# Two routed expert layers: smaller blocks of rows for the least used experts, experts sorted by count in both layers, and weight units of two neighbouring rows per partition

## The chip, the cores and the metric

One core of one Trainium2 chip runs the whole program as one launch. The metric is the device time of one execution in microseconds (us), the median of the runs. Three runs of the kernel before gave 2294.69 us (2292.59 to 2294.75).

## The reference

A diffusion backbone of two layers on 512 latent tokens and 256 context tokens of 1024 features. Layer 0 has a mixer of gated linear recurrence and differential attention, layer 1 one of windowed attention; each is followed by a mixture of 16 experts, of which every token takes two. Layer 0's experts see all 768 tokens, layer 1's the 512 latent ones. The change is in the experts:

```python
def routed_moe(h2d, router_w, router_b, w_gate, w_up, w_down):
    ...
    wts = wts / jnp.sum(wts, axis=-1, keepdims=True)
    ...
    def expert_block(args):
        xblk, e = args
        hid = jax.nn.silu(xblk @ w_gate[e]) * (xblk @ w_up[e])
        return hid @ w_down[e]

    yb = lax.map(expert_block, (xb, block_e)).reshape(n_rows, d_)
    out = jnp.zeros((n_tok + 1, d_), F32).at[row_tok].add(yb * row_w[:, None])
    return out[:n_tok]
```

All numbers are float32. Each of an expert's three weights is 1024 x 1024, 4 MB, so a layer's experts have 201 MB of weights. How many tokens an expert gets depends on the data and is known on the chip only after the router. The result is `x + g2 * f`, and after layer 1 a norm over the features.

## The kernel before, in words

**Precision.** The experts' float32 products are made of three products of parts: `split` (L170 to L197) takes a raw weight from DRAM apart into a high part of 12 bits (ScalarE, L190) and the rest (VectorE, L192), `parts` (L1179) does the same with tokens (`xh`, `xl`) and hidden values (`hh`, `hl`), and `mm3` (L204) issues the products high x high, high x low and low x high, one matmul each (L205 to L207).

**Slots and blocks.** The experts of a layer stand in 16 slots. A slot has room for one block of 128 rows (tokens), or for two. `slot_plan` (L38) gives layer 0 two slots of two blocks, 5 and 11, so 18 blocks; expert 0 always has slot 0, and the others are ranked by their counts on the chip, the two largest in the slots of two blocks. In layer 1 slot s is expert s, with one block each. What doesn't fit in a slot's rows goes to overflow blocks, run by a loop on the device (`For_i`, L1691) whose count comes from the data. A block always takes all of its 128 rows through the matmuls, however many are tokens.

**Steps.** A slot has twelve steps, one for each unit of weights of 1 MB (`load`, L1224). Steps 0 to 3 are gate, gate, up, up for the left 512 columns of the hidden features, 4 to 7 the same for the right 512; such a unit has four groups of 128 rows and 512 columns, a row of 2 KB for each. Steps 8 to 11 are the down weights, two groups of 128 rows and 1024 columns. Each step has twelve matmuls of 512 columns for each block, four for each of the three products, 144 in a slot of one block. The loop over the steps is written so that a unit is split while the one before is multiplied. What follows a product is put off to later steps by a table `late`: `at(step, False, fn)` for the vector engines, `at(step, True, fn)` for TensorE. So the silu product of a half (`hidden`, L1242) is computed in the step after, its four transposes come behind that step's matmuls, and its parts one step later. A block's tokens are fetched from DRAM by an indirect DMA in GpSimd's queue (`fetch`, L1158, `gather`, L1197), transposed by TensorE (`transpose4`, L1173, matmul on L1176) and split. A block's result is weighted and stored to the table YD in DRAM by GpSimd's queue (`result`, L1313, store on L1324), one row of 1024 for each place of a block.

**Loads.** Raw units lie in rings of buffers of 1 MB (strings FIRST and ROUND name the pool that each unit takes). In layer 0, 11 buffers go round, in layer 1, 15. SyncE issues the loads in order (L161), each as soon as its buffer is free. AHEAD lists the units that are loaded before the first tokens are known: twelve of slot 0, and in layer 1 three of slot 1, on GpSimd's queue.

**Ends.** The results of all slots but the last are picked up for each token by indirect gathers from YD (`fetch_y`, L1110), in layer 0 two gathers for each of two early tiles of 128 tokens into `ye` (multiplied by the gate on L1683, added to the stream on L1687), in layer 1 two for each of four tiles that add straight into the stream `xs`. The last slot's block (`direct`, L1284) goes to its tokens without YD: a matmul with a matrix of ones at the tokens' places (`pick`, P on L1280), L1305, is added to the stream on L1306. In layer 1 each tile is then normed and written out (`finale`, L1264). Rows of YD that no slot writes, the overflow's, are set to zero during layer 0's mixer by 14 stores of 512 KB from a small tile `z` (L770).

## Time and profile before

| | |
|---|---|
| runs before | 2294.69 us, the median of 3 (2292.59 to 2294.75) |
| the profiled execution's span, first to last instruction | 2290.2 us |
| TensorE (PE) busy | 2132.9 us, 93% of the span, 11809 matmuls |
| VectorE (DVE) busy | 1702.7 us, 74% |
| ScalarE (ACT) busy | 1381.4 us, 60% |
| GpSimd (POOL) busy | 202.4 us, 9% |
| moved by DMA | 571.26 MB, mean 249 GB/s |
| mean granted TensorE clock | 0.970 |
| splits of weights on DVE (L192) | 822 of 1217 ns, 977.0 us |

The profile is one execution. Times of stages are from the span's start; the runs' median is 4.5 us above this span. Averages over the span hide that the two expert parts have limits of their own, so the stages are read apart. "Busy" of PE counts matmuls, PEld loads of the matmul's stationary operand, which run beside them. A clock of 1.00 is TensorE's upper level of 2.4 GHz, 0.50 its lower level of 1.2 GHz.

### The profile page before, as it was taken

The page shows a single profiled execution, that of the slowest core. Times are in us where ns is not written, and L with a number is a line of the kernel's source. Part 1 is how long each engine was busy: PE and PEld are TensorE (multiplying, and loading weights), DVE is VectorE, ACT ScalarE, POOL GpSimd, SP SyncE. Part 2 cuts the span into 40 slices and gives each one's busy share as a digit, 9 for nine tenths or more (in the row PEclk, how much of TensorE's full clock was granted, in tenths as well). Part 3 has the DMA queues.
Part 4 walks back from the last instruction along what each step waited for, and adds up shares of the span by engine and source line. Part 5 has one row for each costly group of instructions (what it writes and reads, how often), then busy time and mean ns, then how long its engine had stood idle before and what let it go on. Part 6 is the DMA issues. An engine that isn't in the chain of part 4 may idle for free.

```text
span 2290.2 us, 32247 instructions
## 1 busy us (share of the span) xinstructions
PE 2132.9 (93%) x11809; PEld 1717.3 (75%) x11809; DVE 1702.7 (74%) x2506; ACT 1381.4 (60%) x2069; POOL 202.4 (9%) x248
## 2 busy tenths in 40 slices
PE   4899999998969999999999789999979999999997
PEld 2777899996748878888888567566758877777775
DVE  3566646657789975999579865565589988888896
ACT  5344574443348764888478652565368777777774
POOL 2011020000100000000000320000110000000003
PEclk8899999999979999999999899999989999999998
DMA  8556332213689995999699552330489999999985
GB/s 312 199 183 219 87 96 80 75 39 99 227 305 361 375 370 196 380 390 387 225 332 381 185 153 111 148 130 1 167 340 392 388 373 371 372 370 367 375 298 119
DMA packets 244029, 571.26 MB, mean 249 GB/s; under 512 B 12438, under 2 KB 48160, under 8 KB 237720
## 3 DMA queue, kind: packets, MB, share of 16 engines
q1 hardware_dynamic: 215024, 480.24, 57.6%
q0 software_dynamic: 21728, 73.78, 9.8%
q10 hardware_dynamic: 7112, 15.10, 2.0%
q8 instruction: 96, 1.57, 0.3%
q14 instruction: 69, 0.57, 0.1%
HBM read 532.26 MB, written 36.81 MB: 248 GB/s over the span
## 4 chain that ended last, share of the span: by engine, by line
PE 78%; issue 8%; DVE 6%; ACT 4%; DMA 3%; POOL 1%; ACTq 0%; DVEq 0%; SPq 0%; POOLq 0%
PE acc L207 20%; PE acc L205 20%; PE acc L206 20%; PE tp L1176 3%; PE po L1087 2%; PE acc L245 2%; PE big L1021 2%; DVE wl L192 2%; PE acc L1073 1%; PE pair L662 1%; ACT wh L190 1%; PE acc L697 1%; PE acc L647 1%; POOL rr L150 1%; PE big L552 1%
## 5 line engine op out<-in xcount | busy, mean ns | idle before, releaser
L192 DVE TENSOR_TENSOR wl<-raw,wh 128x1024 fp32r<-128x1024 f32 (+1 forms) x822 | 977.0, 1217 | 166.3 <-ACT wh L190 150.6
L190 ACT ACTIVATE wh<-raw 128x1024 fp32r<-128x1024 f32 (+1 forms) x822 | 848.2, 1054 | 276.8 <-PE acc L207 239.2
L205 PE MATMUL acc<-wh,xh 128*128 128x512 f32 x1088 | 437.5, 403 | 0.0
L206 PE MATMUL acc<-wl,xh 128*128 128x512 f32 x1088 | 436.1, 401 | 0.9 <-DVE wl L192 0.8
L207 PE MATMUL acc<-wh,xl 128*128 128x512 f32 x1088 | 432.1, 397 | 0.0
L207 PE MATMUL acc<-wh,hl 128*128 128x512 f32 (+2 forms) x888 | 331.7, 376 | 12.9 <-DVE hl L1181 11.0
L205 PE MATMUL acc<-wh,hh 128*128 128x512 f32 (+2 forms) x888 | 328.0, 381 | 3.9 <-ACT hh L464 3.9
L206 PE MATMUL acc<-wl,hh 128*128 128x512 f32 (+2 forms) x888 | 331.0, 375 | 0.0
L206 PEld LDWEIGHTS acc<-wl,xh 128*128 128x128 f32 x1088 | 206.1, 189 | 52.8 <-DVE wl L192 7.4
L207 PEld LDWEIGHTS acc<-wh,xl 128*128 128x128 f32 x1088 | 205.9, 189 | 48.1 <-DVE xl L1181 0.5
L205 PEld LDWEIGHTS acc<-wh,xh 128*128 128x128 f32 x1088 | 205.8, 189 | 47.0 <-ACT xh L1180 0.5
L207 PEld LDWEIGHTS acc<-wh,hl 128*128 128x128 f32 x888 | 167.8, 190 | 45.3 <-DVE hl L1181 15.8
L205 PEld LDWEIGHTS acc<-wh,hh 128*128 128x128 f32 x888 | 169.2, 191 | 29.0 <-ACT hh L464 4.3
L206 PEld LDWEIGHTS acc<-wl,hh 128*128 128x128 f32 x888 | 168.4, 191 | 28.3 <-DVE wl L192 3.6
L1160 POOL DMA_INDIRECT xg<-H,rowi x32 | 43.9, 1370 | 615.5 <-PE tp L1176 552.9
L150 POOL TENSOR_TENSOR rr<-rv,mhalf 128x1 f32<-128x1 f32 (+1 forms) x54 | 39.1, 724 | 487.9 <-DVE rv L148 470.2
L1026 DVE TENSOR_REDUCE mx<-big 128x1 f32<-128x512 f32 (+1 forms) x64 | 48.1, 756 | 37.1 <-PE big L1024 36.4
L1180 ACT ACTIVATE xh<-tp 128x512 fp32r<-128x512 f32 x68 | 38.9, 588 | 50.2 <-PE tp L1176 30.1
L1028 ACT ACTIVATE ex<-big,mx 128x512 f32<-128x512 f32 (+1 forms) x64 | 47.2, 738 | 33.2 <-DVE mx L1027 32.9
L205 PE MATMUL acc<-hh,wh 128*128 128x384 f32 x192 | 66.5, 346 | 0.8 <-DVE ya L705 0.8
L1180 ACT ACTIVATE hh<-tp 128x512 fp32r<-128x512 f32 x68 | 39.6, 588 | 43.3 <-PE tp L1176 43.3
L206 PE MATMUL acc<-hl,wh 128*128 128x384 f32 x192 | 65.5, 341 | 0.0
(397 smaller groups left out, 3097.5 us busy)
## 6 DMA issues: line engine op xcount, KB each, us to landing
raw<-in_moe_w_up_dram SPq DMA_DIRECT2D x127, 1024.0 KB, 7.7
raw<-in_moe_w_down_dram SPq DMA_DIRECT2D x127, 1024.0 KB, 7.0
raw<-in_moe_w_gate_dram SPq DMA_DIRECT2D x126, 1024.0 KB, 7.9
raw<-in_ada_w_dram SPq DMA_DIRECT2D x48, 1024.0 KB, 6.5
YD<-y POOLq DMA_DIRECT2D x33, 512.0 KB, 6.8
raw<-in_even_w_in_dram SPq DMA_DIRECT2D x40, 256.0 KB, 4.7
YD<-z POOLq DMA_DIRECT2D x14, 512.0 KB, 12.5
raw<-in_even_w_in_dram SPq DMA_DIRECT2D x12, 512.0 KB, 4.2
```

The costliest lines, as they stand in the source:

```text
L150: G.tensor_tensor(r, v, mhalf[:, :n], OP.pow)
L190: S.activation(v[0], src, AF.Copy)
L192: newest[0] = V.tensor_sub(v[1], src, v[0].bitcast(FT))
L205: T.matmul(o, xh, wh, start=start, stop=False)
L206: T.matmul(o, xh, wl, start=False, stop=False)
L207: T.matmul(o, xl, wh, start=False, stop=stop)
L245: T.matmul(ps[32 * i:32 * i + 32], cT[:, k], raw[:, 0, 512 * i:512 * i + 512], start=k % burst == 0, stop=k != kb and k % burst == burst - ...
L1021: T.matmul(ps[:, o0:o1], qT, kT[:, x, k0:k0 + o1 - o0], start=x == 0, stop=x == 1 and not ms, skip_group_check=True)
L1026: V.tensor_reduce(mx[:, i:i + 1], ps[:, :n], AX.X, OP.max, negate=True)
L1028: S.activation(e[:, :n], ps[:, :n], AF.Exp, scale=0.125, bias=mx[:, i:i + 1], accum_out=sm[:, i:i + 1])
L1176: T.transpose(pt[:, i], src[:, 128 * i:128 * i + 128], ident)
L1180: S.activation(oh, pt, AF.Copy)
```

## The change

**Sizes.** A class Plan takes for each slot the number of rows of its blocks. Layer 0: fourteen slots have a block of 128, of which slots 5 and 11 have a further one of 32 rows instead of 128; slots 8 and 15 have 64 rows alone. Layer 1: slots 0, 1, 2, 4, 6, 8, 10, 12, 14 have 128 rows, slots 3, 5, 7, 9, 11, 13 and 15 have 64. In both layers the experts but 0 are ranked by their counts.

**Thin blocks.** A block of 64 or 32 rows isn't split. Its tokens and the raw weights are multiplied in float32, one matmul instead of three, and two (or four) matmuls for different columns of the weights stand side by side in TensorE's array (`thin`, `tile_position`). A slot that is thin alone has twelve steps of one unit each, gate 0 to 3, up 4 to 7, down 8 to 11, and no split; its hidden values (`hidden_thin`) are computed at the end of step 7 at once and not put off. Its result is stored in two or four pieces (`store_rows`). A table of the row's tokens and weights that is repeated for the pieces (`again`) comes from one matmul per size.

**Units.** A unit is now 256 rows by 1024 columns of a weight, with two neighbouring rows on one partition, 8 KB in one run. A whole slot's gate and up steps take halves of the columns of two units each, so all eight units are used in steps 0 to 3 and again in steps 4 to 7. To match, the transposes take every second column (`turned` in place of `transpose4`).

**Order.** Layer 1 loads ahead only slot 0's twelve units; each further slot's expert is read by SyncE from the sorted list. The zeroing of YD covers the thin blocks' rows too, as one store and 21 copies from the rows that it cleared. In layer 0 the blocks' tokens have two buffers instead of three.

```diff
-SLOTS = [slot_plan(2), (None, [1] * 16)]
-AHEAD = [(range(11), range(11, 12)), (range(12), range(12, 15))]
+AHEAD = [(range(11), range(11, 12)), (range(12), range(0))]
...
+PLANS = [
+    Plan([(128,)] * 5 + [(128, 32)] + [(128,)] * 2 + [(64,)] + [(128,)] * 2 + [(128, 32)] + [(128,)] * 3 + [(64,)]),
+    Plan([(128,)] * 3 + [(64,), (128,)] * 6 + [(64,)]),
+]
...
-                    for i in range(min(nbs), max(nbs) + OVMAX):
-                        G.dma_start(YD[128 * i:128 * i + 128, :].rearrange("p (a b) -> p a b", a=4), z[:, None, :].to_broadcast([128, 4, 256]))
+                    clear = sorted(thin | set(range(min(nbs), max(nbs) + OVMAX)))
+                    G.dma_start(YD[128 * clear[0]:128 * clear[0] + 128, :].rearrange("p (a b) -> p a b", a=4), z[:, None, :].to_broadcast([128, 4, 256]))
+                    def clear_next(n):
+                        for b in clear[1 + 2 * n:3 + 2 * n]:
+                            G.dma_start(YD[128 * b:128 * b + 128, :], YD[128 * clear[0]:128 * clear[0] + 128, :])
...
+                def turned(src):
+                    m, k = src.shape[0], src.shape[1] // 128
+                    pt = tp([128, k, m])
+                    v = src.rearrange("p (u x j) -> p u j x", x=128, j=2)
+                    for i in range(k):
+                        T.transpose(pt[:, i], v[:, i // 2, i % 2], ident[:m, :m])
...
+                def thin(ps, x, w, start, stop):
+                    m = x.shape[1]
+                    n = 8 * m
+                    for r in range(128 // m):
+                        T.matmul(ps[m * r:m * r + m, :n], x, w[:, n * r:n * r + n], start=start, stop=stop, tile_position=(0, m * r))
...
-                        w = (wg, wu, wd)[q // 2 % 2 if q < 8 else 2]
-                        w = w[ds(e, 1)].rearrange("o (k p) n -> p (o k) n", p=128)
-                        if q < 8:
-                            return unit(w[:, 4 * (q % 2):4 * (q % 2) + 4, 512 * (q // 4):512 * (q // 4) + 512], i, eng, order)
-                        return unit(w[:, 2 * (q - 8):2 * (q - 8) + 2, :], i, eng, order)
+                        w = (wg, wu, wd)[q // 4][ds(expert(s), 1)].rearrange("o (u p j) n -> p (o u) (j n)", p=128, j=2)
...
+                        rs = [unit(12 * s + 4 * m + 2 * kh + x) for x in range(2)]
+                        return [w for r in rs for w in split(r[:, :, 512 * c:512 * c + 512])], rs
...
+                    def hidden_thin(p, step):
+                        pg, pu = p["ps"]
...
+                        if step is None:
+                            vec()
+                            turn()
+                            store()
...
+                                elif p["m"] < 128 and q == (3 if whole else 7):
+                                    if whole:
+                                        hidden_thin(p, i + 1)
                                     else:
+                                        at(i, True, lambda p=p: hidden_thin(p, None))
...
-                    if one:
-                        base, top = C("base1"), C("top1")
+                    es_ = tt(inner(rank), outer(C(f"order{li}")), OP.is_equal, q3)
+                    V.tensor_copy(esi, red(tt(es_, inner(e16), OP.mult, q3), OP.add, q2))
...
-                        slots.append((e, [r // 128 for r in rows], [slice(r, r + 128) for r in rows]))
-                    gen = run(slots)
+                    gen = run([(lambda s=s: nc.sync.value_load(esi[0:1, s:s + 1], min_val=0, max_val=15)) if s else 0 for s in range(16)],
+                              plan.blocks, plan.sizes)
```

**The order of the instructions, at three places.** On SyncE, which issues the loads, where layer 1's experts begin (`raw` is a buffer of a unit; the names behind the arrow are the weights in DRAM). Before:

```order
L161 DMA raw<-in_moe_w_gate_dram 128x4x512 x2
L161 DMA raw<-in_moe_w_up_dram 128x4x512 x2
L161 DMA raw<-in_moe_w_gate_dram 128x4x512 x2
L161 DMA raw<-in_moe_w_up_dram 128x4x512 x2
L161 DMA raw<-in_moe_w_down_dram 128x2x1024 x4
```

And now:

```order
L158 DMA raw<-in_moe_w_gate_dram 128x2048 x4
L158 DMA raw<-in_moe_w_up_dram 128x2048 x4
L158 DMA raw<-in_moe_w_down_dram 128x2048 x4
L1726 TENSOR_LOAD esi
L1726 ISA x2
```

The four gate units come ahead of the four up units, each with one run per partition, and slot 1's expert number is read from the sorted list (`esi`) before its first load.

On TensorE in layer 1, where before one slot's work runs on (`xh`, `xl`: a block's tokens in parts; `sg`: the silu product; `tp`: a transpose's target). Before:

```order
L205 MATMUL acc<-wh,xh 128x512
L206 MATMUL acc<-wl,xh 128x512
L207 MATMUL acc<-wh,xl 128x512
L1176 MATMUL tp<-ct,sg 128x128 x4
L205 MATMUL acc<-wh,xh 128x512
```

And now, over a thin slot between two whole ones (`xn`, `hn`: its tokens and hidden values, `xg` with a number: the next block's tokens):

```order
L204 MATMUL acc<-wh,hl 128x512
L1203 MATMUL acc<-raw,xn 64x512 x32
L1185 MATMUL tp<-ct,xg_16381 128x128 x4
L1185 MATMUL tp<-ct,sg 128x128 x4
L1203 MATMUL acc<-raw,hn 64x512 x4
L1185 MATMUL tp<-ct,xg_16381 128x128 x4
L1203 MATMUL acc<-raw,hn 64x512 x12
L202 MATMUL acc<-wh,xh 128x512
```

A thin slot is 48 matmuls from raw weights in place of 144 from split ones; the transposes of `sg` stand right ahead of the matmuls that need them, with none of its own slot's between.

On VectorE at the end of layer 0's experts (`ye`: results gathered for an early tile; `y`: the last slot's rows; names with a number are the stream's tiles and gates). Before:

```order
L1254 TENSOR_TENSOR sg<-sg,acc 128x512
L192 TENSOR_TENSOR wl<-raw,wh 128x1024 x3
L1181 TENSOR_TENSOR hl<-tp,hh 128x512
L192 TENSOR_TENSOR wl<-raw,wh 128x1024 x2
L1683 TENSOR_TENSOR ye<-ye,g_12052 128x1024 x2
L1293 SCALAR_TENSOR_TENSOR y<-acc,roww,g_12052 128x512 x2
```

And now:

```order
L189 TENSOR_TENSOR wl<-raw,wh 128x1024 x2
L1371 TENSOR_SCALAR P<-ct,again_5964 128x128 x2
L1795 TENSOR_TENSOR ye<-ye,g_11691 128x1024 x2
L1334 TENSOR_TENSOR sg<-sg,acc 128x512
L1195 COPY hn<-tp 128x2x2x64
L1388 SCALAR_TENSOR_TENSOR y<-acc,again_5964,g_11691 64x512 x2
```

Before, the products of `ye` stand behind the last slot's splits; now, with no split in that slot, they stand ahead of its silu product.

## Rows read from the trace of the kernel before

**Rows 1.** Windows: stretch, length, busy us by engine, clock, DMA share, GB/s.
```profile
core 0: us, PE busy (x) PEld busy (x) DVE busy (x) ACT busy (x) POOL busy (x), PEclk, DMA share, GB/s
...
650.00:1300.00 650.00, 642.86 (x2896) 519.97 (x2897) 540.89 (x539) 470.18 (x525) 37.43 (x42) 0.99 0.90 330
1682.00:2222.00 540.00, 529.98 (x2395) 424.22 (x2395) 487.92 (x482) 405.55 (x447) 31.88 (x29) 1.00 1.01 376
1700.00:1800.00 100.00, 100.00 (x463) 81.77 (x462) 93.65 (x92) 79.79 (x87) 7.52 (x7) 1.00 1.03 392
```

**Rows 2.** Instructions by line and shape: count, busy us, mean ns, idle before.
```profile
L205 PE MATMUL acc<-wh,xh 128*128 128x512 f32 x1088 | 437.5, 403 | 0.0
...
L1176 PEld LDWEIGHTS tp<-ct,xg 128*128 128x128 f32 x272 | 35.1, 145 | 21.1 <-issue 12.3
```

**Rows 3.** SyncE's timeline in layer 0: start, duration, loads of down weights.
```profile
832.77 10.35 SPq L161 DMA_DIRECT2D raw<-in_moe_w_down_dram  x4
...
937.81 8.73 SPq L161 DMA_DIRECT2D raw<-in_moe_w_down_dram  x4
...
973.02 8.71 SPq L161 DMA_DIRECT2D raw<-in_moe_w_down_dram  x4
```

**Rows 4.** The same in layer 1, with the last loads.
```profile
1877.28 9.29 SPq L161 DMA_DIRECT2D raw<-in_moe_w_down_dram  x4
...
1914.07 9.29 SPq L161 DMA_DIRECT2D raw<-in_moe_w_down_dram  x4
...
2215.08 2.64 SPq L161 DMA_DIRECT2D raw<-in_moe_w_down_dram  x2
```

**Rows 5.** TensorE's timeline: float32 matmuls of other parts; L1305 is of full width.
```profile
1417.29 3.64 PE L245 MATMUL acc<-raw,cT 128*32 128x512 f32 x32 [0.51 <-DVE rp L334]
...
1473.37 1.51 PE L1087 MATMUL po<-at,vt 128*64 128x256 f32 x10
...
2267.22 7.13 PE L1305 MATMUL acc<-y,P 128*128 128x512 f32 x16 [0.39 <-DVE y L1293]
```

**Rows 6.** Timeline of layer 1's experts, start and end, four engines.
```profile
1675.74 0.42 DVE L1493 TENSOR_TENSOR q<-r,ct 128x256 f32<-128x256 f32 x1
...
1681.58 0.79 PE L205 MATMUL acc<-wh,xh 128*128 128x512 f32 x1
...
2231.68 0.53 POOL L1324 DMA_DIRECT2D YD<-y  x1 [36.23 <-DVE y L1321]
...
2235.79 1.65 POOL L1110 DMA_INDIRECT xs<-YD,dse  x1 [3.04 <-DMA YD<-zero]
...
2252.12 1.77 POOL L1110 DMA_INDIRECT xs<-YD,dse  x1 [0.30 <-issue]
...
2275.63 0.68 DVE L1306 TENSOR_TENSOR xs<-xs,acc 128x512 f32<-128x512 f32 x1
```

**Rows 7.** Timeline of GpSimd and VectorE at the end of layer 0's experts.
```profile
1265.89 0.53 POOL L1324 DMA_DIRECT2D YD<-y  x1 [34.66 <-ACT y L1323]
...
1279.96 1.68 POOL L1110 DMA_INDIRECT ye<-YD,dse  x1 [1.24 <-DMA ye<-YD,dse]
...
1294.93 2.35 DVE L1683 TENSOR_TENSOR ye<-ye,g 128x1024 f32<-128x1024 f32 x2
```

**Rows 8.** DMA issues: count, KB each, median us from issue to landing.
```profile
YD<-z POOLq DMA_DIRECT2D x14, 512.0 KB, 12.5
...
ye<-YD,dse POOLq DMA_INDIRECT x4, 6.7
...
xs<-YD,dse POOLq DMA_INDIRECT x8, 7.8
```

**Rows 9.** Windows: the start, while modulation weights of 8 KB per partition are loaded.
```profile
14.00:22.00 8.00, 5.99 (x38) 5.75 (x39) 2.92 (x5) 8.00 (x12) 1.65 (x3) 1.00 1.01 427
```

**Rows 10.** DMA queues, 1700 to 2200 us: packets, MB, share of 16 engines.
```profile
q0 software_dynamic: 3989, 14.52, 7.8%
```

**Rows 11.** Windows: 10 us after TensorE had stood idle.
```profile
100.00:105.00 5.00, 2.84 (x10) 2.24 (x11) 1.41 (x3) 2.34 (x5) 0.00 (x0) 0.50 0.02 3
105.00:110.00 5.00, 5.00 (x37) 2.34 (x37) 2.96 (x4) 1.45 (x4) 0.35 (x1) 0.88 0.30 74
```

More of the change, by code (lines that the diff above doesn't have):

```diff
@@ L1222, in gather @@
                         at(first, False, get)
-                        for q in range(2):
+                        for q in range(2 if m == 128 else 1):
                             at(step + q, True, lambda q=q: turn(q))
                             at(step + 1 + q, False, lambda q=q: store(q))
-                    jobs = [(e, [dict(row=r, x=x) for x, r in enumerate(rows)], bs) for e, bs, rows in slots]
-                    ahead = {}
-                    def weights(i):
-                        return split(ahead.pop(i) if i in ahead else load(i))
@@ L1234, in load @@
-                    def load(i, eng=nc.sync, order=False):
-                        s, q = divmod(i, 12)
-                        e = jobs[s][0]
+                    slots, n = [], 0
+                    for s in range(len(experts)):
+                        slots.append([])
+                        for b, m in zip(blocks[s], sizes[s]):
+                            r0 = (b + NB) * 128 if in_loop else b * 128
+                            row = (lambda i, k, r0=r0: ds(r0, 128)) if in_loop else (lambda i, k, r0=r0: slice(r0 + i, r0 + i + k))
+                            slots[-1].append(dict(b=b, m=m, n=n, row=row))
+                            n += 1
@@ new lines, in part, with unit @@
+                    def part(m, kh, c):
+                        w = (wg, wu)[m][ds(expert(0), 1)].rearrange("o (u p j) n -> p (o u) j n", p=128, j=2)
+                        raw = room[1 + one].tile([128, 2048], FT, name="raw", tag="raw").rearrange("p (k n) -> p k n", k=4)
+                        for x in range(2):
+                            nc.sync.dma_start(raw[:, 2 * x:2 * x + 2], w[:, 2 * kh + x, :, 512 * c:512 * c + 512])
+                        return raw
+                    def unit(u):
+                        if u not in raws:
+                            raws[u] = ahead.pop(u) if u in ahead else load(u)
+                        return raws[u]
@@ L1249, in vec, with hidden @@
+                    def hidden(p, c, step):
+                        pg, pu = p["ps"]
                         def vec():
                             if c == 0:
-                                blk["h"] = [(wk2 if blk["x"] else wk).tile([128, 8, 128], FR, name=x, bufs=1) for x in ("hh", "hl")]
+                                p["h"] = [wk.tile([128, 8, 128], FR, name=x, bufs=1) for x in ("hh", "hl")]
                             sg = wk.tile([128, 512], FT, name="sg", bufs=1 if one else 2)
@@ L1296, in vec, with store_rows, direct @@
+                    def store_rows(p, y):
+                        if p["m"] == 128:
+                            G.dma_start(YD[p["row"](0, 128), :], y)
+                        else:
+                            for _, rows, at_, cs in pieces(p):
+                                G.dma_start(YD[p["row"](0, p["m"]), cs], y[rows, at_])
+                    def direct(p, step):
+                        def vec():
+                            p["y"] = gated(p)
                             if not one:
-                                G.dma_start(YD[blk["row"], :], y2)
@@ L1371, in run @@
-                            for blk in blocks:
-                                if q in (3, 7):
-                                    hidden(blk, c, i + 1)
+                            last = s == len(slots) - 1
+                            split_, as_is = ws
+                            for p in ps_:
+                                if q in (0, 4, 8) and p["m"] == 128 or q == 0:
+                                    p["ps"] = [acc(), acc()]
+                                elif q == 8:
+                                    p["ps"] = [acc()]
@@ L1376, in run @@
                                 elif q == 11:
-                                    (direct if last else result)(blk, i + 1)
+                                    (direct if last else result)(p, i + 1)
                             ws = nws
@@ L1485, in tl @@
                         if n == 256:
-                            return rp.tile(shape, dt, name="q3", bufs=1 if one else 3)
+                            return rp.tile(shape, dt, name="q3", bufs=3)
                         if n in (16 * nt, 96) and not hold:
@@ L1652, in ffn @@
                     next(gen)
+                for m in sizes:
+                    rep = wk.tile([128, 512], FT, name="rep", tag="sg", bufs=1 if one else 2)[:, :128]
+                    V.tensor_copy(rep.rearrange("p (r m) -> p r m", m=m), ident[:, None, :m].to_broadcast([128, 128 // m, m]))
+                    pd = tp([128, 2, NB])
+                    T.matmul(pd, rep, tab, start=True, stop=True)
+                    V.tensor_copy(again[m], pd)
                 if BRIEF[li]:
```

327 lines of the change are left out of this document (180 added, 147 removed).

## The prediction

> **What bounds the kernel now.** I read the busy time by stage first, then the counts, then SyncE's timeline, whose loads mark the pace of the expert slots. The two expert stages are more than half of the span: layer 0's from 655 to about 1300 us, layer 1's from 1682 us to the end. In both TensorE is busy nearly throughout at a clock of 1.00, and in layer 1 the DMA engines are too, at 376 GB/s [rows 1]. The 1088 matmuls of one kind on gathered tokens are 34 blocks of 32: 18 blocks of 128 rows in layer 0 and 16 in layer 1, and no overflow block [rows 2]. A slot of one block takes 35.2 us in layer 0 (973.02 less 937.81) and up to 36.8 us in layer 1 (1914.07 less 1877.28); the stretch from 832.77 to 937.81 holds a two-block slot and a single one, so two blocks take 105.0 - 35.2 = 69.8 us [rows 3, 4]. TensorE sets these times. The DMA engines are close behind it: a slot moves 12.6 MB of weights and 1.05 MB of tokens and results, 36.3 us at 376 GB/s. So a cheaper slot helps only down to the time of its loads, and what the change does to the loads counts as much as what it does to the matmuls.
>
> **No overflow after the change.** From the reference's inputs I worked out the tokens of each expert. Layer 0: expert 0 has 110, the others in order 145, 129, 113, 112, 110, 105, 98, 95, 88, 87, 83, 80, 76, 55, 50. The new slots hold 128 for expert 0, then 160, 160, eleven times 128, and 64, 64. Layer 1: 21, then 122, 106, 98, 94, 82, 71, 69, 69, 53, 50, 46, 45, 35, 34, 29, for nine slots of 128 (expert 0's among them) and seven of 64. All fit.
>
> **A thin slot's matmuls.** A unit of 256 rows by 1024 columns takes 12 matmuls now. For 64 rows it takes four in float32, two side by side; for 32 rows eight of half the width, four side by side. Two rows show the price of such work. 32 float32 matmuls of 512 columns, four side by side, took 3.64 us, and ten of 256 columns, two side by side, 1.51 us; a full-width float32 one took 7.13/16 = 0.45 us [rows 5]. So 512 columns cost 3.64/8 = 0.45 us by the first, 2 x 1.51/5 = 0.60 by the second, and the same 0.45 where nothing stands beside them. A 64-row unit is two such pairs, 0.9 to 1.2 us; I take 0.95, nearer to the row with as many columns, so 11.4 us for a slot of 12 (upper end 14.4). To this come an estimated 3.4 us in which TensorE waits for silu, product and transposes between steps 7 and 8, which here are not put off (the like of it takes 0.4 to 0.8 us each in the rows: 0.68 for a vector instruction of 512 columns [rows 6], 0.59 for four transposes at 145 ns [rows 2]). Together 14.8 us against 35.2. A 32-row block costs about half, 5.2 us, plus an estimated 0.8 for its transposes.
>
> **Layer 0.** The two slots of two blocks become 35.2 + 6 = 41.2 us: 2 x (69.8 - 41.2) = **57 us** less. Slot 8 falls to 14.8 us, but the next whole slot needs eight units in its first four steps, and at some 2.6 us each (below) these come 26 us after slot 8 starts; of the 20 us I keep **10** (ends 4 and 15). Slot 15 gains little. VectorE's order there puts the products of the early tiles (ye) ahead of this slot's own silu product, since no split follows that would hold them back. The ye gathers were queued behind slot 14's store at 1265.89, the fourth was issued at 1279.96 and landed some 7 us later, and the products ran at 1294.93 [rows 7, 8]. Now VectorE stands until about 23 us after slot 14's end, and the slot takes 23 + 2.4 + 3 + 3.6 = 32 us: **2 us** less (up to 14 if the gathers land sooner). The 14 whole slots have as many matmuls as before. Together **69 us**.
>
> **The loads.** Now a partition reads 2 KB runs (gate, up) or 4 KB (down); then every unit is one run of 8 KB per partition. The trace of before has that shape: the modulation weights. While they alone were loaded, the engines moved 427 GB/s at a share of 1.01, against 376 at the same share in layer 1 [rows 1, 9]. I take 427 for weights: 29.5 us per slot. Of the other traffic, 7.8% of 500 us went to 14 slots' gathers and results, 2.8 us each [rows 10]; seven of 16 slots now move half, so 2.2 us. Sum 31.7 us, **2.64 us per unit**. Lower end: no gain from longer runs, 392 GB/s for everything, the rate where the queue was fullest [rows 1]: 13.4 MB per slot, 2.85 us per unit. A page of the Trainium skill, DMA: Bandwidth & Descriptors (section Where 436 GB/s comes from), says that for loads from HBM the HBM side binds at about 358 GB/s. By it a slot takes 37.4 us, estimated from that figure, layer 1 would gain only some 15 us, and the time would be about 2213 us. The trace disagrees: it shows 376, 392 and 427.
>
> **Buffers.** A whole slot now reads its eight gate and up units twice, in steps 0 to 3 and 4 to 7, and frees them only from step 3 on. In layer 0 the ring has 11 buffers: the next slot's eight units can be asked for 12 to 24 us after this slot's start and take 21 us, so the last is there by some 36 us; it is needed 41 us after. In layer 1 there are 15. So I cost holding at nothing; the cover is those 5 us.
>
> **Layer 1.** Experts are sorted there now, so slot 1's units wait for the sorted list instead of being loaded ahead by GpSimd, and about ten vector instructions like the one at 1675.74 stand before expert 0's tokens are split: 0 to 6 us, I take 2; the first matmul moves from 1681.6 to 1683.6 [rows 6]. Slots 0 to 2 are whole, 35.2 to 36.8 us each: until 1791.6. The ring then allows units up to 50; 141 are left. Thirteen slots, seven thin: matmuls need 6 x 36 + 7 x 14.8 = 320 us, loads 141 x 2.64 = 372. So the loads bind and end at 2164, against 2222 [rows 1, 4]. Slot 14's eighth unit is the 16th from the end, 2122; a split and nine steps later the slot ends, about 2151. The tail is next late: slot 14's store was issued at 2231.68, eight adding gathers went out from 2235.79 to 2252.12 and landed some 8 us later [rows 8], about 28 us after the store, hidden under the last slot's 35 us [rows 6]. Now that slot is short and the gathers are not covered: its store goes out at 2153, and 28 us later is 2181; I add 9 us, two thirds of the 13 us of loads that are still under way then, since the gathers share the DMA engines with them: 2190. From the last tile's sum to the end it is 2290.2 - 2275.6 = 14.6 us. The end comes at 2205: **85 us** less.
>
> **Small terms.** Transposes now load every second column: 0 if the weight load still hides (145 ns each [rows 2]), 38 us if it doubles and all shows (17 matmul-bound slots, 16 each, 0.14 us). I take 0, as in the rows that load runs beside the matmul before it. The zeroing of the result table was 14 stores of 12.5 us [rows 8]; now one store and 21 copies in GpSimd's queue during the mixer, where the DMA engines have room (the share was 0.30 at 105 us [rows 11]): 0. At worst one step waits for one landing of that size, 12.5 us; at best one that waited for a store before no longer does, 12.5 us the other way.
>
> **Sum.** 69 + 85 = 154; 2290.2 - 154 = 2136 us of span. The median of the runs, 2294.69, lies 4.5 us over that span: **2140 us**.
>
> **Rivals.**
> *Loads get no faster* (2.85 us per unit): loads end 30 us later, slot 9 loses 3: 2173. For: the longer run is shown in 8 us of the trace only, with little else going on. Against: rate per share is plain there.
> *The clock drops.* Thin slots leave TensorE idle in pieces; after such a stretch it was granted 0.50, its lower level of 1.2 GHz, from 100 to 105 us and 0.88 over the next 5 us of full work [rows 11]. If each whole slot behind a thin one (seven) does its first four steps at that level and one more: at most 4 us each beyond the pace of the loads, 28 in all, 2168. The Trainium skill, TensorE: Matmul & The Clock Gate (section HAM oscillation — how this bites in real kernels), describes the same: a matmul loop that waits for DMA in every round starts every round at the lower clock. No stretch of this trace has such a loop at full length.
> *Pieces do not run side by side*: a 64-row slot costs 21 us, still under its loads, but layer 0 loses 2 x 16 + 10: 2182. Rows 5 speak against it.
> *Everything a little better*: loads at the highest share, gathers unhindered: 2115.
> *Held buffers starve the loads* (slower): if the next slot's eight units come late, each of the 23 whole slots waits. From 6.7 us per slot (154/23) the change loses; at 10 us it gives 2370. That needs 4 us or more per unit where rows 1 show 2.8.
> *The change doesn't do what it says*: an expert over its slot costs a further block, some 45 us: 2185. The counts speak against it.
>
> **Chances.** Forecast 0.52 (its own range 2115 to 2170), slower loads 0.20, clock 0.12, better 0.05, not side by side 0.03, overflow 0.03, starved loads 0.05. The range 2105 to 2215 takes in all but the starved loads, some of the best case, and the transposes' upper end on top of a rival. Below 0.2% (4.6 us) a measurement can't tell a difference; faster 0.94, same 0.01, slower 0.05.
>
> **What would show it.** Right: slots 5 and 11 of layer 0 at 41 us; thin slots of layer 1 with TensorE waiting for loads, a pair of whole and thin at 63 us; 420 GB/s or more there; ye's products ahead of slot 15's silu product in layer 0, and some 20 us at the end in which the gathers are awaited. Wrong: whole slots over 37 us in layer 0 (held buffers, transposes), a rate at 390, a clock of 0.5 through whole slots, or an overflow block.

## The result, and the profile after

| | before | after |
|---|---|---|
| median of the runs, same chip (4 each) | 2293.64 us | 2198.69 us (2195.63 to 2201.97) |
| ratio | | 0.9589, 95% interval 0.9574 to 0.9604 |
| span of the profiled execution | 2290.2 us | 2197.3 us |
| first product of layer 0's experts | 655.60 | 653.13 |
| last slot's product with P, layer 0 | 1298.30 | 1257.22 |
| first product of layer 1's experts | 1681.58 [rows 6] | 1642.06 |

The marks that no row ahead shows, on TensorE's timeline, of the kernel before:

```profile
655.60 0.79 PE L205 MATMUL acc<-wh,xh 128*128 128x512 f32 x1
...
1298.30 3.70 PE L1305 MATMUL acc<-y,P 128*128 128x512 f32 x8 [0.16 <-DVE y L1293]
```

And of the changed kernel:

```profile
653.13 0.79 PE L202 MATMUL acc<-wh,xh 128*128 128x512 f32 x1
...
1257.22 2.77 PE L1418 MATMUL acc<-y,P 64*128 64x512 f32 x8 [0.85 <-DVE y L1388]
...
1642.06 0.79 PE L202 MATMUL acc<-wh,xh 128*128 128x512 f32 x1
```

The change gains 95 us where 154 were forecast: faster, inside the range, with a time 59 us above the forecast. By the marks of the table, layer 0's experts went from 642.7 to 604.1 us, **38.6 us** less (forecast 69); layer 1's, up to the end of the span, from 608.6 to 555.2 us, **53.4 us** less (forecast 85). What lies ahead of the experts and between the layers moved by 2.5 us less and 1.6 more.

The costliest groups of the page after, part 5 (busy us, mean ns of one), answer to [rows 2]:

```profile
L202 PE MATMUL acc<-wh,xh 128*128 128x512 f32 x736 | 294.6, 404 | 3.4 <-ACT wh L187 3.4
...
L1203 PE MATMUL acc<-raw,xn 128*64 128x512 f32 (+1 forms) x832 | 141.3, 529 | 0.0
```

736 is 23 whole blocks of 32: 14 in layer 0, nine in layer 1, no overflow. The thin blocks' count is the key to what follows. For gate and up the program issues 32 of these matmuls for a slot of 64 rows and 64 for a block of 32, so 9 x 32 + 2 x 64 = 416; the trace has 832. A float32 matmul leaves **two** records.

The loads in the same stretches as before, by windows (columns as in [rows 1]):

```profile
core 0: us, PE busy (x) PEld busy (x) DVE busy (x) ACT busy (x) POOL busy (x), PEclk, DMA share, GB/s
...
1642.00:1700.00 58.00, 53.75 (x246) 42.25 (x244) 52.72 (x77) 41.78 (x47) 4.57 (x4) 0.99 0.76 298
1700.00:1800.00 100.00, 95.89 (x432) 66.51 (x431) 69.97 (x70) 57.59 (x64) 6.59 (x7) 1.00 0.99 403
...
1800.00:2100.00 300.00, 282.91 (x1255) 175.46 (x1255) 166.31 (x171) 131.56 (x150) 20.25 (x22) 0.98 1.01 412
```

The engines move 412 GB/s at the share at which they moved 376. But TensorE is busy 283 of 300 us. Unlike the forecast, next to nothing waits for loads: from 1760 to 2146 us ScalarE's splits wait 1.6 us in all for a unit to land. One turn of a thin slot in layer 1 shows why (TensorE's timeline; `xn` gate and up, `hn` down, then the next whole slot's first two products, the second of which needs the low part `wl` of a split):

```profile
1821.76 13.95 PE L1203 MATMUL acc<-raw,xn 128*64 128x512 f32 x64
1835.64 0.74 PE L1185 MATMUL tp<-ct,xg 128*128 128x128 f32 x4
1836.58 0.74 PE L1185 MATMUL tp<-ct,sg 128*128 128x128 f32 x4 [0.19 <-DVE sg L1334]
1837.79 1.94 PE L1203 MATMUL acc<-raw,hn 128*64 128x512 f32 x8 [0.47 <-ACT hn L1194]
...
1840.34 5.37 PE L1203 MATMUL acc<-raw,hn 128*64 128x512 f32 x24
1845.64 0.51 PE L202 MATMUL acc<-wh,xh 128*128 128x512 f32 x1
1848.60 0.80 PE L203 MATMUL acc<-wl,xh 128*128 128x512 f32 x1 [2.46 <-DVE wl L189]
...
1887.13 13.95 PE L1203 MATMUL acc<-raw,xn 128*64 128x512 f32 x64
```

Gate and up, 16 pairs of matmuls, take 13.95 us, so 0.87 us per pair; the thin slot takes 23.9 us up to the next slot's first product and 26.8 us up to its second (forecast 14.8), and a pair of a whole and a thin slot 65.4 us (1887.13 less 1821.76). At the end TensorE idles 2.46 us for a split. VectorE's timeline has the reason: the weighted result of the thin slot stands ahead of the splits, in order, and waits for the thin slot's last matmul.

```profile
1845.76 1.53 DVE L1388 SCALAR_TENSOR_TENSOR y<-acc,again,g 64x512 f32<-64x512 f32 x2 [3.99 <-PE acc L1203]
1847.32 4.63 DVE L189 TENSOR_TENSOR wl<-raw,wh 128x1024 fp32r<-128x1024 f32 x4
```

In layer 0, by SyncE's loads of down weights as in [rows 3], a two-block slot and a single one span 85.9 us (916.62 less 830.73), where it was 105.0:

```profile
830.73 25.35 SPq L158 DMA_DIRECT2D raw<-in_moe_w_down_dram  x4
...
916.62 19.82 SPq L158 DMA_DIRECT2D raw<-in_moe_w_down_dram  x4
...
952.14 12.46 SPq L158 DMA_DIRECT2D raw<-in_moe_w_down_dram  x4
...
1016.06 21.30 SPq L158 DMA_DIRECT2D raw<-in_moe_w_down_dram  x4
```

The single slot is 35.5 us (952.14 less 916.62), so a two-block slot 50.4. The last pair of rows spans slot 8 and a whole one: 63.9 us, two whole ones before 70.4. Layer 0's end, VectorE, answers to [rows 7]:

```profile
1241.49 1.23 DVE L1795 TENSOR_TENSOR ye<-ye,g 128x1024 f32<-128x1024 f32 x1 [25.42 <-DMA ye<-YD,dse]
1244.11 1.23 DVE L1795 TENSOR_TENSOR ye<-ye,g 128x1024 f32<-128x1024 f32 x1 [1.39 <-DMA ye<-YD,dse]
1245.25 0.68 DVE L1334 TENSOR_TENSOR sg<-sg,acc 128x512 f32<-128x512 f32 x1
```

VectorE stands 25 us for the gathers ahead of the last slot's silu product, whose matmuls had ended at 1232.8. TensorE waits 13.18 us of these, and the down matmuls behind take 8.78 us:

```profile
1245.99 1.13 PE L1185 MATMUL tp<-ct,sg 128*128 128x128 f32 x4 [13.18 <-DVE sg L1334]
1247.59 8.78 PE L1203 MATMUL acc<-raw,hn 128*64 128x512 f32 x32 [0.47 <-ACT hn L1194]
```

### The profile page after: what moved, and what is told of

Its sections match the earlier page's. It is cut to its first block, busy times and chain, and to the rows that moved or that the text cites. A ratio compares the mean times of both kernels' runs of the same rounds, so it can differ in the third digit from the quotient of the medians.

```text
span 2197.3 us, 31169 instructions
## 1 busy us (share of the span) xinstructions
PE 1990.3 (91%) x11431; PEld 1493.5 (68%) x11431; DVE 1428.8 (65%) x2281; ACT 1144.3 (52%) x1816; POOL 203.6 (9%) x267
## 4 chain that ended last, share of the span: by engine, by line
PE 76%; issue 8%; DVE 6%; DMA 4%; ACT 3%; POOL 1%; ACTq 0%; DVEq 0%; SPq 0%; POOLq 0%
PE acc L203 17%; PE acc L202 16%; PE acc L204 16%; PE acc L1203 9%; PE tp L1185 3%; PE po L1091 2%; PE acc L242 2%; PE big L1025 2%; DVE wl L189 2%; PE acc L1077 1%; PE pair L659 1%; PE acc L694 1%; POOL rr L146 1%; PE acc L644 1%; DMA yg<-YD,dsi 1%
## 5 line engine op out<-in xcount | busy, mean ns | idle before, releaser
L189 DVE TENSOR_TENSOR wl<-raw,wh 128x1024 fp32r<-128x1024 f32 (+1 forms) x605 | 718.5, 1215 | 131.8 <-ACT wh L187 124.8
L187 ACT ACTIVATE wh<-raw 128x1024 fp32r<-128x1024 f32 (+1 forms) x605 | 628.2, 1054 | 248.6 <-PE acc L204 202.0
L203 PE MATMUL acc<-wl,xh 128*128 128x512 f32 x736 | 298.9, 406 | 28.5 <-DVE wl L189 28.1
L202 PE MATMUL acc<-wh,xh 128*128 128x512 f32 x736 | 294.6, 404 | 3.4 <-ACT wh L187 3.4
L204 PE MATMUL acc<-wh,xl 128*128 128x512 f32 x736 | 293.5, 399 | 0.0
L203 PE MATMUL acc<-wl,hh 128*128 128x512 f32 (+2 forms) x704 | 259.5, 369 | 0.0
L204 PE MATMUL acc<-wh,hl 128*128 128x512 f32 (+2 forms) x704 | 259.1, 369 | 0.3 <-DVE hl L462 0.3
L204 PEld LDWEIGHTS acc<-wh,xl 128*128 128x128 f32 x736 | 140.2, 190 | 32.0 <-DVE xl L1190 0.5
L1203 PE MATMUL acc<-raw,xn 128*64 128x512 f32 (+1 forms) x832 | 141.3, 529 | 0.0
L1203 PE MATMUL acc<-raw,hn 128*64 128x512 f32 (+1 forms) x416 | 75.6, 541 | 4.3 <-ACT hn L1194 4.3
```

What stands on the lines that cost most here:

```text
L187: S.activation(v[0], src, AF.Copy)
L189: newest[0] = V.tensor_sub(v[1], src, v[0].bitcast(FT))
L202: T.matmul(o, xh, wh, start=start, stop=False)
L203: T.matmul(o, xh, wl, start=False, stop=False)
L204: T.matmul(o, xl, wh, start=False, stop=stop)
L1203: T.matmul(ps[m * r:m * r + m, :n], x, w[:, n * r:n * r + n], start=start, stop=stop, tile_position=(0, m * r))
```

## The experiments

Two theories were set against each other for layer 1: **A**, TensorE binds it, since float32 matmuls cost twice what was assumed; **C**, the loads bind it. Further ones bear on the runs of the loads (D, E) and on held buffers (F). Times are compared by their ratios to the kernel before, run beside them on the same chip; differences in us are between medians, and the changed kernel's 2198.69 us is the reference for them.

### One side of the pairs left out

```diff
                     for r in range(128 // m):
+                        if m == 64 and r and not (start or stop):
+                            continue
                         T.matmul(ps[m * r:m * r + m, :n], x, w[:, n * r:n * r + n], ...)
```

> Edit: in the slots of 64 rows the second of the two matmuls that stand side by side is left out, but for the first and the last of each sum of eight. Left out of the computation: three quarters of the right halves of those slots' products. In the changed kernel the gate and up matmuls of such a slot take 13.95 us in one piece. Theory A (the two run side by side, and a float32 matmul of 512 columns takes 0.87 us, alone or beside another): the piece stays at 13 to 14 us, the span within 0.5%. Theory B (they run one behind the other at 0.44 us each): the piece falls by three eighths to 8.7 us, and the span by some 40 to 50 us. Theory C (layer 1's pace is set by the loads): the span stays even if the piece gets shorter.

Measured: 2206.25 us in a single run (0.3% more), and the piece, on TensorE's timeline of this kernel:

```profile
1762.17 13.95 PE L1205 MATMUL acc<-raw,xn 128*64 128x512 f32 x40
```

40 records in place of 64, and the same 13.95 us. The second matmul of a pair costs nothing: they do stand side by side. And 13.95/16 = 0.87 us is what one costs with nothing beside it.

### Half of the thin blocks' matmuls

```diff
-                                            thin(o, (p["x"] if q < 8 else p["h"])[:, kk], raw[:, j], kk == 0, kk == 7)
+                                            if j == 0:
+                                                thin(o, (p["x"] if q < 8 else p["h"])[:, kk], raw[:, j], kk == 0, kk == 6)
```

> Edit: thin blocks (64 and 32 rows) multiply only every second group of 128 input features, so they have half as many float32 matmuls, which gives them the price that the prediction had assumed, 0.45 us per 512 columns; all else stays. Left out: half of each sum of the thin blocks. Theory A (the price of these matmuls is the mis-sized term): layer 0 gets back some 12 us for its two 32-row blocks, slot 8 about 5; in layer 1 TensorE then waits for loads, a pair of a whole and a thin slot falls from 64.7 to 62 to 63.5 us, and the end of layer 1 comes some 15 to 25 us earlier; the whole time falls by 35 to 50 us, to 2150 to 2165. Theory C (the loads set layer 1's pace already): the pair stays at 64 to 65 us, and the time falls by 15 to 22 us only, from layer 0.

Measured: 2177.15 us, ratio 0.9488 (0.9472 to 0.9504), 21.5 us less. Starts of the thin slots in layer 1:

```profile
1743.95 4.51 PE L1203 MATMUL acc<-raw,xn 128*64 128x512 f32 x20
...
1798.22 4.51 PE L1203 MATMUL acc<-raw,xn 128*64 128x512 f32 x20
...
1862.67 4.51 PE L1203 MATMUL acc<-raw,xn 128*64 128x512 f32 x20
...
2121.66 4.51 PE L1203 MATMUL acc<-raw,xn 128*64 128x512 f32 x20
```

The first pair takes 54.3 us, all later ones 64.1 to 65.3 (1862.67 less 1798.22 is the first of them), with waits for weights in each: ScalarE's splits wait 88 us for units from 1760 to 2146 us, where it was 1.6. That is C: at the price that the prediction assumed, the loads bind, at 64.7 us per 24 units, 2.69 us each. Layer 1 gets only 7.2 us shorter (548.0). Layer 0 gets 16.5 us shorter. Its two-block slots fall by 4.8 us each, to 45.6 (833.63 to 914.87 on this kernel's SyncE, less 35.6), and its last slot from 37.3 to 29.9, while slot 8 and the whole slot behind it take 63.5 us where they took 63.9. With half the matmuls ScalarE's splits wait 11.7 us for loads there, which now decide; in the changed kernel none of them waits for a load.

### Runs of 4 KB, and of 2 KB

```diff
-                        w = (wg, wu, wd)[q // 4][ds(expert(s), 1)].rearrange("o (u p j) n -> p (o u) (j n)", p=128, j=2)
+                        w = (wg, wu, wd)[q // 4][ds(expert(s), 1)].rearrange("o (u j p) n -> p (o u) j n", p=128, j=2)
...
-                    v = src.rearrange("p (u x j) -> p u j x", x=128, j=2)
+                    v = src.rearrange("p (u j x) -> p u j x", x=128, j=2)
```

> Edit: a unit still has 256 rows by 1024 columns and the same number of DMAs, but its two rows on a partition are 128 rows apart, so each partition reads two runs of 4 KB instead of one of 8 KB, and the transposes take neighbouring columns. Theory D (the long runs give the loads their 410 GB/s in layer 1, against 375 before): the rate falls to 380 to 395 GB/s, layer 1 takes 10 to 25 us longer, the time 2210 to 2220. Rival E (the rate comes from fewer DMAs under way or less other traffic, not from the runs): the rate stays at 410 and the time within 0.3%. Apart from that, if the transposes of every second column cost anything, a whole slot of layer 0 falls from 35.6 to 35.2 us, some 6 us over the layer.

Measured: 2198.57 us, ratio 0.958 (0.9561 to 0.9598): no difference. For 2 KB, the layout of the change is kept and each load is cut into its column halves:

```diff
+                        rc = raw.rearrange("p (j c n) -> p c j n", j=2, c=2)
+                        for c in range(2):
+                            d = eng.dma_start(rc[:, c], w[:, q % 4, c])
```

> Edit: each unit's load is cut into two DMAs of one column half each, so the runs are 2 KB as the gate and up loads of the kernel before had them; what lies where in the chip's memory, the holding of buffers and all else stay (8 KB in the changed kernel, 4 KB in the second run). Theory D, in the form that is left after the 4 KB run (the loss comes between 4 and 2 KB): the rate in layer 1 from 1800 to 2100 us falls from 412 to 370 to 390 GB/s, pairs take 68 to 71 us, and the time grows by 25 to 45 us. Rival E (the run's length doesn't matter): pairs of 64 to 65 us and the time within 0.4%.

Measured: 2230.53 us, ratio 0.9725 (0.9709 to 0.9741), 31.8 us more; layer 1 alone takes 32.3 us longer (587.5 against 555.2). From 1800 to 2100 us, the 4 KB run and then the 2 KB run:

```profile
1800.00:2100.00 300.00, 282.45 (x1266) 171.71 (x1266) 165.45 (x170) 132.55 (x153) 16.04 (x22) 0.98 1.03 404
```

```profile
1800.00:2100.00 300.00, 276.88 (x1200) 172.74 (x1201) 170.37 (x173) 137.50 (x154) 19.72 (x21) 0.99 1.05 384
```

412, 404 and 384 GB/s for 8, 4 and 2 KB, at a full share in each. So the loss that D names shows between 4 and 2 KB, and above 4 KB nothing is left that the time shows. But the 2 KB run also doubles the number of DMAs, and the two weren't parted: that the length of the run is the cause isn't shown. Transposes of every second column against neighbouring ones cost 0.14 us per whole slot (35.62 against 35.48), next to nothing.

### No slots of 64 rows

```diff
-    Plan([(128,)] * 5 + [(128, 32)] + [(128,)] * 2 + [(64,)] + [(128,)] * 2 + [(128, 32)] + [(128,)] * 3 + [(64,)]),
-    Plan([(128,)] * 3 + [(64,), (128,)] * 6 + [(64,)]),
+    Plan([(128,)] * 5 + [(128, 32)] + [(128,)] * 5 + [(128, 32)] + [(128,)] * 4),
+    Plan([(128,)] * 16),
```

> Edit: all slots of 64 rows get 128 rows again, in both layers; the two 32-row blocks, the sorted experts of layer 1 and the 8 KB units stay. If TensorE binds layer 1 (theory A), a whole slot costs some 36 us where a thin one costs 27: seven slots lose 9 each, 63 us less what the thin slots lose around them (2.5 to 4 us each): 40 to 60 us longer in layer 1. In layer 0 slot 8 costs about 8 more and slot 15 stays or gains (no wait for the gathers ahead of its silu product): 0 to 10. Together 2235 to 2265. If instead the loads bind (theory C), layer 1 gets longer only as far as whole slots exceed the loads' pace of 32 us: 16 x 35.5 = 568 against 555, and the time is 2205 to 2225.

Measured: 2244.73 us, ratio 0.9799 (0.9774 to 0.9823), 46 us more, as A has it. Layer 1 takes 605.6 us, only 3.0 less than before the change. Its slots all take 35.55 us, where 36.8 were the rule before [rows 4]. From 1800 to 2100 us TensorE is busy throughout and the DMA engines, at 0.95, are not:

```profile
1800.00:2100.00 300.00, 300.00 (x1355) 244.07 (x1354) 277.77 (x272) 235.38 (x254) 16.68 (x16) 1.00 0.95 384
```

From the down loads of slot 1 to those of slot 15 it is 499.0 us where it was 510.1. These 11 us are no gain from the loads: before, nothing waits for a load in that stretch, but TensorE waits ten times, 10.0 us in all, for the low part `hl` of the hidden values on VectorE, and never for it here; which part of the change did away with that wasn't tested. Slot 0 gives back 6.5 (48.5 us from the first product to its store, before 42.0).

### The two orders on VectorE

```diff
-                        at(step, False, lambda: store_rows(p, (gated if one else weighted)(p)))
+                        def vec():
+                            with tc.issue_after(newest[0].ins) if p["m"] < 128 and not in_loop else nullcontext():
+                                y = (gated if one else weighted)(p)
+                            store_rows(p, y)
+
+                        at(step, False, vec)
```

> Edit: the weighted result of a thin slot (y) is ordered behind the four splits of the next whole slot on VectorE (and on ScalarE in layer 0), not ahead of them. In the changed kernel VectorE waits with it for the thin slot's last matmul, and TensorE then idles 2.46 us at each of six whole slots of layer 1 that follow a thin one. Theory A (TensorE binds layer 1): each pair gets 2.5 to 4 us shorter (the idle time and the slower clock behind it), 15 to 24 us in all, and the time falls to 2175 to 2185. Theory C (the loads bind it at 64.5 us a pair, as the run with half the thin matmuls showed): the 2.46 us are gone, but TensorE waits for loads as long instead; pairs stay at 64 to 65 us, and the time falls by 0 to 6 us.

Measured: 2191.38 us, ratio 0.9556 (0.954 to 0.9572), 7.3 us less; the two intervals miss each other by very little, and the traces agree (layer 1 548.5 us). The thin slots' starts give both theories their part: 61.2 and 61.5 us for the second and third pair, 64.7, 65.4 and 64.0 for the fourth to sixth.

```profile
1815.11 13.95 PE L1203 MATMUL acc<-raw,xn 128*64 128x512 f32 x64
1876.32 9.23 PE L1203 MATMUL acc<-raw,xn 128*64 128x512 f32 x42
...
2002.53 12.67 PE L1203 MATMUL acc<-raw,xn 128*64 128x512 f32 x58
...
2067.91 12.67 PE L1203 MATMUL acc<-raw,xn 128*64 128x512 f32 x58
```

TensorE alone would need 61.2 us; it runs into the loads' 64.7 after three pairs (ScalarE's splits wait 26 us for units from 1937 to 2132 us, 1.3 from 1760 to 1937). In the changed kernel the waits on VectorE had made its pairs, 64.7 us on average, as long as the loads need, almost without a wait for a load. So A holds for the changed kernel, and C sets in as soon as TensorE gets faster.

The second order, at layer 0's end (`late_mul[0]` is the last instruction that makes the slot's `y`):

```diff
...
-                    for t in EARLY:
-                        with tc.issue_after(newest[0].ins):
-                            V.tensor_mul(ys[t], ys[t], g2[0])
                 finish(gen)
                 if not one:
                     for t in EARLY:
+                        with tc.issue_after(late_mul[0].ins):
+                            V.tensor_mul(ys[t], ys[t], g2[0])
+                    for t in EARLY:
```

> Edit: in layer 0's last slot the products of the early tiles (ye) are ordered behind the slot's own silu product, hidden values and result on VectorE, where the changed kernel has them ahead and TensorE waits 13.2 us. If that wait is what makes the slot longer than the 32.4 us that it took before: TensorE's gap falls to about 1 us, the down matmuls run at the upper clock (8.78 us to 7.1), layer 0 ends 11 to 15 us earlier and the time falls to 2184 to 2189. Rival: the gathers are needed right after anyway, so the wait moves to the sums behind the result, and the time falls by less than 4 us.

Measured: 2188.9 us, ratio 0.9545 (0.953 to 0.9561), 9.8 us less. The last slot on TensorE, in this kernel:

```profile
1217.49 13.95 PE L1203 MATMUL acc<-raw,xn 128*64 128x512 f32 x64
1232.30 0.75 PE L1185 MATMUL tp<-ct,sg 128*128 128x128 f32 x4 [0.86 <-DVE sg L1334]
1233.53 7.09 PE L1203 MATMUL acc<-raw,hn 128*64 128x512 f32 x32 [0.47 <-ACT hn L1194]
1241.46 2.77 PE L1418 MATMUL acc<-y,P 64*128 64x512 f32 x8 [0.85 <-DVE y L1388]
```

The gap is gone, and the down matmuls take 7.09 us in place of 8.78. From slot 14's store to this last product it is 22.9 us, 14.4 less than in the changed kernel, and layer 0 is 13.2 us shorter; the medians differ by less. The profiled execution is the fastest of this kernel's four, 5.3 us under their median; more isn't known of it.

### Slot 0 of layer 1 in quarters, and all three together

```diff
+                        if one and not in_loop and s == 0 and q < 8:
+                            w = (wg, wu)[q // 2 % 2][ds(expert(0), 1)].rearrange("o (u p j) n -> p (o u) j n", p=128, j=2)
...
+                                d = eng.dma_start(raw[:, 2 * x:2 * x + 2], w[:, 2 * (q % 2) + x, :, 512 * (q // 4):512 * (q // 4) + 512])
```

> Edit: in layer 1's slot 0 alone the gate and up units are quarters of 512 rows by 512 columns again, each used in one step and then free, where the changed kernel holds eight units of 256 by 1024 until steps 4 to 7; bytes and all other slots stay. Theory F (holding slot 0's units keeps the loads of the ring waiting at the start of layer 1, 0.80 of the engines' time in the first 60 us where it is 1.01 later, and layer 1 never gets that back because the loads bind it): the share in those 60 us rises to 0.9 to 1.0, and the time falls by 6 to 15 us. Theory A (TensorE binds layer 1, or is level with the loads): the loads run ahead, TensorE's pace stays, and the time falls by less than 4 us.

Measured: 2199.35 us, ratio 0.9587 (0.9568 to 0.9607): nothing. The share in the first 58 us rises from 0.76 to 0.83 only, not to the 0.9 that F asks for, and the time stays: buffers that slot 0 holds are not what costs time here.

> Edit: all three together: y behind the splits, ye behind the last slot's result in layer 0, slot 0 of layer 1 in quarters. If loads and TensorE are level in layer 1, the first and the third only show together: the sum of the three single gains and 5 to 15 us on top, 2160 to 2178. If the loads alone bind it: the sum of the single gains, 2175 to 2185.

Measured: 2179.5 us, ratio 0.9497 (0.9481 to 0.9513), 19.2 us less, near the sum of the single gains (16.4).

> Edit: the two orders alone (y behind the splits, ye behind the last slot's result), without the quarters in slot 0, which gave nothing alone. The single gains were 7.3 and 9.8 us: 2180 to 2184, level with the run of all three, if the quarters are worth nothing; 2184 or more if they were worth the 3 us that all three had over the sum.

Measured: 2177.88 us, ratio 0.9495 (0.9479 to 0.9511): without the quarters the same.

### Thin slots spread from the second slot on

This run has the two orders as well; only the new part of its edit is shown.

```diff
...
-    Plan([(128,)] * 3 + [(64,), (128,)] * 6 + [(64,)]),
+    Plan([(128,), (64,), (128,), (64,), (128,), (64,), (128,), (128,), (64,), (128,), (64,), (128,), (128,), (64,), (128,), (64,)]),
```

> Edit: the two orders, and in layer 1 the seven thin slots stand at 1, 3, 5, 8, 10, 13 and 15 and no longer at every second place from 3 on, so that TensorE takes units faster than whole slots do (2.3 us per unit against 3.0) from the second slot on, and the ring of 15 buffers never fills for long. If the loads bind layer 1 from its start to its end (180 units at 2.69 us are 484 us, where the run with y behind the splits needed some 503 from the sorted list to the last unit): the share in the first 120 us rises to 1.0, the last unit lands 8 to 19 us earlier, and the time is 2163 to 2174. If TensorE binds as much (nine whole slots of 35.5 and seven thin ones of 25): within 4 us of the run with the two orders alone.

Measured: 2171.74 us, ratio 0.9465 (0.9441 to 0.9489), 27 us under the changed kernel. Most of that is the two orders; against the run with these alone it is 6.1 us, the lowest median of all, with intervals that overlap. The traces agree with a gain: layer 1 takes 542.8 us, 548.8 with the orders alone. Starts of thin slots:

```profile
1731.65 13.95 PE L1203 MATMUL acc<-raw,xn 128*64 128x512 f32 x64
...
1889.48 13.95 PE L1203 MATMUL acc<-raw,xn 128*64 128x512 f32 x64
...
1951.30 13.96 PE L1203 MATMUL acc<-raw,xn 128*64 128x512 f32 x64
```

The last two are a pair apart, 61.8 us, so this late TensorE is held up by less than a microsecond, where the last three pairs with the orders alone took 64.2 to 65.1. In the changed kernel three whole slots in a row at the start (2.96 us per unit on TensorE, 2.69 in the loads) leave the ring full and the DMA engines idle: a share of 0.76 from 1642 to 1700 us above. With thin slots early the share is 0.84 from 1632 to 1700 us (0.80 with the two orders alone) and 1.01 from 1700 to 1750 (0.97). Over the first 120 us of layer 1 it comes to 0.91 against 0.88, short of the 1.0 that was expected.

## Why the prediction was right in its direction and 59 us too low

- **No overflow**: right, 23 whole blocks in the records.
- **A thin slot's matmuls**: the step that failed. "So 512 columns cost 3.64/8 = 0.45 us" took the count of records in [rows 5] for a count of matmuls. L1305 there is four tiles by two halves, eight matmuls, under a count of 16. A float32 matmul of 512 columns takes 0.87 us, so gate, up and down of a thin slot take 21 us and not 11.4, and the slot 24 to 27. Side by side was right. The rival "Pieces do not run side by side" named the price of 21 us, so it was near it by luck: the first run refutes its reason.
- **Layer 0**, 69 forecast, 38.6 measured: two-block slots 50.4 us each and not 41.2, 39 us less in place of 57 (half of the miss is the price, by the run with half the matmuls; the rest, other work of the thin block, was put at 0.8 us). Slot 8 with its neighbour 6.5 in place of 10, but not set by loads as argued: no split of that stretch waits for one, and TensorE is as slow there by its price as the loads would be (63.9 us, and 63.5 where loads decide). Slot 15 4.9 us longer (37.3 against 32.4), not 2 shorter: the wait for ye was placed rightly (forecast some 23 us after slot 14's end, the rows show the first product 21.5 us after its store), but the down matmuls behind it, put at 3.6 us, took 8.78: 7.09 is their price at the upper clock, the rest the lower clock. Whole slots, put at no change, took 35.6 us where they took 35.2.
- **The loads**: 2.64 us per unit forecast, 2.69 measured, and not by the 427 GB/s of [rows 9] but by 412. That the new units load faster was right, and runs of 4 KB would have done; that the run's length alone does it isn't shown. The page DMA: Bandwidth & Descriptors of the Trainium skill, in its section Where 436 GB/s comes from, puts the limit of loads from HBM at about 358 GB/s, one core's half of a stack. The 412 GB/s over 300 us here, with one core at work, disagree.
- **Buffers** at nothing: right for the time, as the quarters show in layer 1's slot 0; no run parted it for the other slots.
- **Layer 1**, 85 forecast, 53.4 measured. The sorting, put at 2 us ahead of the first product, cost up to 6 inside slot 0, whose splits stand on VectorE among its instructions (48.2 us from the first product to the slot's store, before 42.0). With the quarters that slot took 44.8 us and the sorting was the same, so the sorting alone isn't shown to cost all of the 6. Slot 3 starts 115.8 us after the first product (1757.81 less 1642.06), not 108. Then "So the loads bind": the sum let TensorE, at 50.8 us per pair, use up a lead of 14 units, which made 59.9 us per pair of the loads' 63.4; the pairs took 64.7, 29 us more over six of them. TensorE needed 61.2 us, and with the wait for the split and the clock behind it 63.9 to 65.5, so no lead was there to use. With the assumed price the pairs would still have taken 63.0 on average (377.7 us for six), so only 10 of these 29 us are the price; the other 19 are the pace (2.69) and a lead that held for one pair only. The loads issue slot 1's units when the sorted list is there: SyncE waits 16.1 us for it, costed at nothing. No run undid that, so what it costs stays open.
- **The end**: gathers hidden or not was a question that fell away, since the last thin slot took 25 us; from its start to the end of the span 51.5 us, forecast 54.
- **The clock** rival: a small part of it was real. TensorE's first product behind the wait at a thin slot's end took 0.65 to 0.80 us in three of six cases where it took 0.50 in the others, and the clock was 0.98 from 1800 to 2100 us; without the wait for the split it is 1.00. The three pairs that hold these slower products took 65.3 to 65.5 us, the other three 63.9, so it is part of those 7.3 us.

## What to carry to other kernels

Before a duration is divided by a count of the trace, check the count against the program's loops: two records per float32 matmul halved the price here. Where two limits come out within a few per cent of each other, as TensorE's 61.2 us and the loads' 64.7 did here, taking work off one shows only until the other binds. After a change removes work that used to sit between two instructions of an in-order engine, read the new order for waits that this work had covered: both orders found here are such.

## What the runs showed of the hardware

- A float32 matmul of 512 columns and 64 output rows took 0.87 us, alone or two side by side; one split product of 512 columns advances TensorE by 0.23 us (1789.66, 1789.89 and 1790.12 are successive starts).
- With weights loaded in runs of 8, 4 and 2 KB the DMA engines of this one core moved 412, 404 and 384 GB/s from 1800 to 2100 us, at a share of 1.01 to 1.05; the 2 KB runs came in DMAs of 512 KB, the others of 1 MB.
- After 13 us in which TensorE waited, in layer 0's last slot, eight pairs of down matmuls took 8.78 us where they take 7.09 without the wait. The windows of the changed kernel show the lower level, 1.2 GHz, in the first five microseconds behind the wait, and the upper one after them:

```profile
1246.00:1251.00 5.00, 4.53 (x12) 1.72 (x14) 0.42 (x1) 0.38 (x1) 0.00 (x0) 0.50 0.48 182
1251.00:1256.00 5.00, 5.00 (x26) 1.54 (x22) 0.00 (x0) 0.00 (x0) 0.00 (x0) 1.00 0.00 0
```
